# A decoder layer in full fp32 on one core: norm rows by a store and a broadcast load, eleven norms' sums by VectorE, half of the last residual transposed by VectorE, squares placed later

## The chip, the cores and the metric

The kernel runs on one core of a Trainium2 chip. The core has TensorE (PE in the profile, with PEld for its weight loads), VectorE (DVE), ScalarE (ACT), GpSimd (POOL) and SyncE (SP), which here only issues DMAs; POOL and ACT issue some too. Each engine works through its own instructions in order, and semaphores tie the engines together. The metric is the time of one execution in microseconds (us), the median of several.

## The reference, cut to what matters

One layer over 1024 tokens of width 1024: a half feed-forward, a mixer (stick-breaking attention of 16 heads beside a Mamba-2 scan, SSD), cross-attention to 256 memory tokens, and a second half feed-forward. Each part has an RMSNorm ahead of it and one behind it.

```python
def rmsnorm(x, g):
    y = x * lax.rsqrt(jnp.mean(x * x, axis=-1, keepdims=True) + EPS)
    return y * g

f = swiglu(rmsnorm(h, ffn1_pre_g), ffn1_w_gu, ffn1_w_down)
h = h + 0.5 * rmsnorm(f, ffn1_post_g)
m = hybrid_mixer(rmsnorm(h, mix_pre_g), ...)
h = h + rmsnorm(m, mix_post_g)
c = memory_cross_attention(rmsnorm(h, xa_pre_g), rmsnorm(mem, mem_g), ...)
h = h + rmsnorm(c, xa_post_g)
f = swiglu(rmsnorm(h, ffn2_pre_g), ffn2_w_gu, ffn2_w_down)
h = h + 0.5 * rmsnorm(f, ffn2_post_g)
...
# in the mixer: o_att = rmsnorm(o_att, attn_norm_g), and y = rmsnorm(y in 2 groups of 512, ssd_norm_g)
```

## The kernel before, in words

Activations lie transposed: 128 of the 1024 features on the partitions, tokens along the free axis, in two halves of 512 tokens (`hh`), so a half is 8 tiles of 128x512 (`d`). Weights and activations are split into a high and a low part (`split`, L267), and a product is three matmuls (`mm3`, L282: high x high, high x low, low x high). The stages in order, with their rough times: `ffn1` up to 440 us, its down projection to 655 (`down1`, L979, by seven products in place of eight, `down7`, L1019), `ssd` to 1000, `attention` to 1545, `mix_out` to 1672, `xattn` to 1923, `ffn2` up to 2357, its down projection to the end at 2581 (`down_rows`, L1140, again `down7`, with tokens on the partitions).

The norm of one half goes in steps. The squares of its 8 tiles are summed to one 128x512 tile (`sumsq`, L361; the sum is `acc`, `yacc`, `asum` or `bh`), still with features on the partitions. `rms_cols` (L322) sums over partitions with PE: for each block of 128 tokens one matmul with the block as weights and a column of constants (`small`) as the moving side, which gives a 128x4 tile in the PSUM bank `ms`, one column for each block of tokens. ACT takes the root, DVE the reciprocal: the column `c` (`cpost`, `cpre`, `ca`, `cy`, `cmem`). `rms_rows` (L346) turns the column to a row that stands on all 128 partitions: four matmuls with the broadcast column as weights and the identity (`ident`) as the moving side, then a copy by ACT from PSUM (L355) to the row `r` (`rpost`, `rpre`, `rn`, `Ct`, `sq`). Both are matmuls in fp32, which PE makes in several passes.

Who uses which: `post` (L386) closes a stage. It multiplies the result `F` by the row `rpost` and the gain (`apply`, L404, L407), adds the residual `XL` (L411), stores the new residual `h` by POOL (L416), splits it for the next stage (L418, L423), sums the squares of the new residual and makes column and row of the next norm (`cpre`, `rpre`). `pre` (L484) does the latter for the stages that don't spread it. `group_norm` (L1525) makes the columns of the two SSD groups, `keys` (L1548) those of the memory; `mix_row` (L1805), `norm_row` (L2058) and `memory_values` turn these to rows where they are used: in the mixer's output projection, which runs in four passes of 8 tiles (half 0: scan part, attention part; then half 1), each tile's bank is emptied by a product with its row (`mix_sum`, L2003 to L2008).

What sets the order: each engine's instructions are placed by a scheduler in the order of a modelled clock (`self.clock`, which PE's work drives). Work that is put off is listed in `self.later` with a time and runs when the clock has come that far; `pinned` puts a group of matmuls at a given time. DMAs on SP stand in the order in which this places them; an SP transfer that must wait holds all that stand behind it.

In the attention, `vtr` (L1736) turns the values of a pair of heads: DVE transposes 32x32 blocks (`dv`), SP stores to DRAM (`vt<-dv`) and loads back in another order with four DMAs (`dv<-vt`, L1731); `kevac` (L1753) empties the keys and has SP move them by four DMAs (`k<-xl`, L1700).

In the last stage the residual `h`, which lies transposed in DRAM, has to come to tokens on the partitions. POOL loads the 8 tiles of a half (`fetch_h`, L1157), PE transposes 128x128 blocks to two PSUM banks (`shift`, L1160, 8 for each block of 128 tokens), and DVE adds (`end`, L1187, the row at L1190). Half 0 is done while the last products run (`early`, L1201), half 1 behind the last product (`last`, L1241). `ssq` (L1167) takes the squares of a row by ACT, `gain` (L1182) multiplies by the gain on DVE, and the sums of the seven products are gathered at L1080 and L1091.

Of the kernel before, what the change touches and what calls it, by code (L numbers as in the profile page):

```python
# [47 lines left out]
class Kern:  # L48
# [273 lines left out]
    def rms_cols(self, groups, c, ones=None, r2=None):  # L322
# [20 lines left out]
        if r2 is not None:  # L343
            self.kp(nc.vector.tensor_tensor(out=c, in0=c, in1=r2, op=ALU.mult))

# [40 lines left out]
    def post(self, hh, gname, r2, gnext=None, out=None, step=None, spread=True, pins=(23000, 28000), accs=None, at=None, tail=None, hold=False, late=None):  # L386
# [10 lines left out]

        def cols():
            self.rms_cols([accs], c, r2=r2)

        def rows():
            self.rms_rows(c, r)
# [25 lines left out]
        if out is None:  # L428
            self.h[hh] = [self.tc.dram_tile([P, H], F32, name=self.nm(f"h{hh}{d}")) for d in range(KT)]
# [36 lines left out]
        if out is None:  # L466
# [4 lines left out]
            self.held = [lambda: self.rms_cols([accs2], c2)]  # L471
            if not hold:
                q.append((t + t1, self.held.pop()))
            if spread:
                q.append((t + t2, lambda: self.rms_rows(c2[:, :], r2_)))
# [8 lines left out]
    def pre(self, hh, accs, t1, t2):  # L484
        c = self.t(self.rp, [P, 4], F32, f"cpre{hh}", bufs=2)
        r = self.t(self.rp, [P, H], F32, f"rpre{hh}", bufs=1)
        with self.pinned(t1):
            self.rms_cols([accs], c)
        with self.pinned(t2):
            self.rms_rows(c[:, :], r)  # L490
        self.R[hh], self.C[hh] = r, c
# [487 lines left out]
    def down1(self, sp, wdn, act_d, xs_d, gpost, gnext):  # L979
# [15 lines left out]
        def finish(m, i):  # L995
# [5 lines left out]
            elif m == 4:  # L1001
# [4 lines left out]
                self.post(0, gpost, self.C[0], gnext, step=2600, accs=accs[:], tail=(20500, 24000), late=38000)  # L1006
# [10 lines left out]
        self.post(1, gpost, self.C[1], gnext, step=2000, accs=accs[:], at=(6500, 9000, 10000), tail=(7500, 10500))  # L1017
# [122 lines left out]
    def down_rows(self, sp, wdn, act_d, xs_d, out):  # L1140
# [16 lines left out]
        def fetch_h(hh, d):  # L1157
            self.kp(nc.gpsimd.dma_start(out=hs[hh][d], in_=self.h[hh][d]))

        def shift(hh, tb):  # L1160

            xt = [self.t(self.mmp, [P, H], F32, "mm") for _ in range(2)]
            for d in range(KT):
                self.tr(xt[d // 4][:, (d % 4) * P : (d % 4 + 1) * P], hs[hh][d][:, tb * P : (tb + 1) * P])
            return xt

# [34 lines left out]
        def early(tb):  # L1201

            root(0, tb)
            xt = shift(0, tb)
            for dh in range(2):
                end(0, tb, dh, xt)

        def finish(m, tb):
            if m == 2:
# [5 lines left out]
                for d in range(KT):  # L1215
                    at(2500 * d, fetch_h, 0, d)
            elif m == 4:
# [6 lines left out]
                for d in range(KT):  # L1224
                    at(1000 + 2500 * d, fetch_h, 1, d)
            elif m == 5:
                for tb in range(4):
                    at(3000 + 5000 * tb, ssq, 1, tb, 0)
                    at(5000 + 5000 * tb, gain, 1, tb, 0)
# [11 lines left out]
        def last(tb):  # L1241
            xt = shift(1, tb)
# [7 lines left out]
    def ssd(self, close):  # L1250

        nc, ap = self.nc, self.ap
        with self.tc.tile_pool(name=self.nm("ssa"), bufs=1, reuse_waits="tile") as ep, \
# [271 lines left out]
            def group_norm(gr):  # L1525
                c = self.norm_c[gr] = self.t(self.rp, [P, 8], F32, f"cy{gr}")
                self.rms_cols([[y] for y in yacc], c, ones=self.ones512)
# [20 lines left out]
            def keys(n0, n1):  # L1548

                mh, ml, acc, rm = env["mem"]  # L1550
                if n0 == 0:
                    self.mem_c = self.t(self.rp, [P, 2], F32, "cmem")
                    self.rms_cols([[acc]], self.mem_c)
                    yield
                for n in range(n0, n1):
                    ps = yield from self.kvproj(next(W), mh, ml)
                    if n == 0:
                        self.rms_rows(self.mem_c[:, :], rm)
# [88 lines left out]
    def attention(self):  # L1647
        nc, ap = self.nc, self.ap
        with self.pools("at", ["o", "a"], ["w"]) as (op, sp, wsp, pp):
# [52 lines left out]
            def inproj(p):  # L1702
# [12 lines left out]
                def steps(hh, t, before):  # L1715
# [14 lines left out]
                    for q in range(4):  # L1730
                        nc.sync.dma_start(  # L1731
                            out=v[32 * q : 32 * q + 32, :].rearrange("e (j c d) -> e j c d", j=4, c=4), in_=rows[q]
                        )
                    return v
# [49 lines left out]
                vtr(1, tv[1])  # L1784
                kevac(evac((yield from last), 1), h1)

            def before(n):
# [7 lines left out]
                if n == 10:  # L1795
                    late.append(mix_row(0))
                if n == 12:
                    late.pop()()
# [6 lines left out]
            def mix_row(i):  # L1805
                self.mix_r.append(self.t(self.rp, [P, H], F32, f"rpre{i}", bufs=1))
                return self.rms_rows(self.norm_c[i][:, 0:4], self.mix_r[i], tr_tile)
# [109 lines left out]
            def memory_values(mh, ml):  # L1917

                rm = self.t(self.tp, [P, H], F32, "sq1")[:, 0:MEM]
                self.rms_rows(self.mem_c[:, :], rm)  # L1920
# [31 lines left out]
            def beside():  # L1952
                late.append(mix_row(1))
                self.first = self.mix_first(ready.pop())
                for n in range(4 * MIXED):
# [3 lines left out]
                    if n == 2:  # L1959
                        late.pop()()  # L1960
# [10 lines left out]
            self.Wo, self.mix_r, ready, late = self.wstream(wo[0:MIXED]), [], [], []  # L1971
# [38 lines left out]
    def mix_out(self):  # L2010
# [3 lines left out]
        with self.pools("mo", ["r", "a"], ["b"]) as (rp, sp, sp2, dnp):  # L2014
# [43 lines left out]
            def norm_row(i, hh, at):  # L2058
                r = self.t(rp, [P, H], F32, f"rn{i}")
                with self.pinned(self.clock + at):  # L2060
                    self.rms_rows(self.norm_c[i][:, 4 * hh : 4 * hh + 4], r)
# [6 lines left out]
            for n, (hh, part) in enumerate(passes):  # L2068
# [3 lines left out]
                def norms(t):  # L2072
                    c = self.norm_c[2] = self.t(self.rp, [P, 4], F32, "ca", bufs=2)
                    with self.pinned(self.clock + t):
                        self.rms_cols([asum[-1:]], c)
# [33 lines left out]
                if n == 1:  # L2109
                    self.run_later(float("inf"))  # L2110
                    self.post(0, "mix_post_g", None, "xa_pre_g", step=5000, spread=False, accs=ends[0], at=(6000, 11500, 14000), tail=(18000, 0))
                    self.resid(1, 5000, 17000)
                if n == 3:
                    self.flush(0)
                    self.post(1, "mix_post_g", None, "xa_pre_g", step=3000, spread=False, accs=ends[1], at=(6000, 10500, 13000), hold=True)


    def xattn(self):
# [3 lines left out]
        with self.pools("xf", ["a", "b", "w"], []) as (sp, sp2, wsp, pp):  # L2122
# [107 lines left out]
            for s in range(8):  # L2230
# [3 lines left out]
                if s == 4:  # L2234
# [6 lines left out]
                    self.post(0, "xa_post_g", None, "ffn2_pre_g", step=5000, at=(8500, 16000, 19000))  # L2241
# [47 lines left out]
    def run(self):  # L2289
        nc, tc, ap = self.nc, self.tc, self.ap  # L2290
        with tc.tile_pool(name="const", bufs=1) as cp, tc.tile_pool(name="state", bufs=1, reuse_waits="tile") as xp, \
# [6 lines left out]
            self.place(cp, 448)  # L2298
# [17 lines left out]
            def consts():  # L2316
                cst = self.t(self.fp, [P, 2, P], F32, "rpost")
                nc.sync.dma_start(out=cst, in_=ap["consts"])
                nc.scalar.copy(self.ident, cst[:, 0, :])
                nc.scalar.copy(self.tri, cst[:, 1, :])  # L2320
# [41 lines left out]
            self.norm_c = {}  # L2362
# [111 lines left out]
```

## Time and profile before

| | us |
|---|---|
| median of 3 runs | 2585.72 |
| lowest and highest run | 2585.55, 2587.47 |
| the profiled execution's own time | 2583.27 |
| its span, first to last instruction | 2581.5 |
| PE busy | 2564.0 (99%) |
| DVE busy | 2000.7 (78%) |
| ACT busy | 1289.0 (50%) |
| POOL busy | 576.5 (22%) |
| mean granted clock of PE | 0.999 |

A row of a profile's group reads: line, engine, operation, output<-inputs, shapes, how often | busy time in us, mean ns of one | idle time of the engine just ahead, and what ended it. A row of the timeline starts with its start and its duration in us; in brackets stand the idle time ahead of it and what ended that. Records of matmuls overlap, so the price of one is read from starts. A row of windows gives the stretch, its length, the busy time of each engine with its count of instructions, the granted clock (1.00 is full speed), the share of the DMA engines and GB/s.

### The profile page before, as it was taken

Reading aid. Unit: us, or ns where it says so; the run is one execution under the profiler, and the core shown is the slowest. Engines: PE = TensorE matmul, PEld = TensorE weight load, DVE = VectorE, ACT = ScalarE, POOL = GpSimd, SP = SyncE. Lnnn points to the kernel's source line nnn. Section 1 sums busy time; section 2 is a strip of 40 time slices with the busy share of each in tenths; the row PEclk is TensorE's granted clock in tenths of the full one; section 3 lists DMA queues with packets and bytes.
Section 4 is the critical chain, followed back from the end, with each engine's and each line's share of the span. In section 5 each row is a group of like instructions: output and inputs, shape, how many; then the busy total and the mean of one; then the engine's idle time right before and its main releaser. Section 6 shows DMA issues by size and latency. Waiting matters only on the chain. (4 is left out here: it accounts for less than half of the span.)

```text
span 2581.5 us, 36855 instructions
## 1 busy us (share of the span) xinstructions
PE 2564.0 (99%) x12786; PEld 2141.0 (83%) x12786; DVE 2000.7 (78%) x3074; ACT 1289.0 (50%) x2302; POOL 576.5 (22%) x674
## 2 busy tenths in 40 slices
PE   9999999999999999999999999999999999999999
PEld 7888888888787778888888898888888888888887
DVE  7988997779689884787787876876656887777777
ACT  7434444555356663555555654455554433334453
POOL 2555553001000001111111110111012655541000
PEclk9999999999999999999999999999999999999999
DMA  6458988655665516666666655547658443327654
GB/s 240 163 180 293 308 290 305 220 185 166 232 205 197 184 72 212 186 177 160 176 171 152 206 167 202 197 155 260 202 185 304 150 162 111 110 82 237 192 175 147
DMA packets 251628, 498.24 MB, mean 193 GB/s; under 512 B 60592, under 2 KB 69168, under 8 KB 251440
## 3 DMA queue, kind: packets, MB, share of 16 engines
q1 hardware_dynamic: 204176, 387.31, 46.4%
q0 software_dynamic: 23360, 65.03, 8.6%
q10 hardware_dynamic: 23904, 43.53, 4.6%
q8 instruction: 101, 1.65, 0.3%
q14 instruction: 87, 0.71, 0.1%
HBM read 331.65 MB, written 143.13 MB: 184 GB/s over the span
## 5 line engine op out<-in xcount | busy, mean ns | idle before, releaser
L139 PE MATMUL mm<-xh,whi 128*128 128x512 f32 x1312 | 516.7, 403 | 1.1 <-DVE ft L668 0.5
L139 PE MATMUL mm<-xh,wlo 128*128 128x512 f32 x1280 | 491.7, 392 | 0.0
L139 PE MATMUL mm<-xl,whi 128*128 128x512 f32 (+1 forms) x1248 | 485.7, 389 | 0.3 <-DVE xl L277 0.3
L139 PEld LDWEIGHTS mm<-xh,wlo 128*128 128x128 f32 x1280 | 240.6, 188 | 52.4 <-DVE wlo L270 0.5
L139 PEld LDWEIGHTS mm<-xh,whi 128*128 128x128 f32 x1312 | 247.0, 188 | 43.1 <-issue 3.9
L139 PEld LDWEIGHTS mm<-xl,whi 128*128 128x128 f32 x1248 | 235.6, 189 | 33.4 <-DVE xl L277 0.8
L1829 DVE TENSOR_TENSOR_SCAN nb<-nb,begin 128x128 f32<-128x128 f32 (+7 forms) x128 | 172.1, 1347 | 32.3 <-ACT nb L1825 31.9
L1825 ACT ACTIVATE nb<-z,scale 128x128 f32<-128x128 f32 (+2 forms) x192 | 109.5, 580 | 89.5 <-PE z L139 88.6
L270 DVE TENSOR_TENSOR wlo<-wraw,whi 128x1024 fp32r<-128x1024 f32 x61 | 74.6, 1223 | 51.3 <-ACT whi L268 50.9
L268 ACT CAST whi<-wraw 128x1024 fp32r<-128x1024 f32 (+1 forms) x77 | 73.9, 959 | 70.4 <-PE mm L139 43.5
L1846 POOL DMA_DIRECT2D mix<-sq x64 | 53.0, 828 | 248.7 <-DVE sq L1844 181.5
L669 ACT ACTIVATE ft<-ft 128x512 f32<-128x512 f32 x88 | 55.5, 632 | 95.5 <-DVE ft L668 94.9
L139 PE MATMUL dn<-xh,wlo 128*128 128x512 f32 x296 | 101.2, 390 | 0.0
L772 POOL TENSOR_TENSOR wc<-raw,wraw 128x512 f32<-128x512 f32 x55 | 80.7, 1467 | 56.4 <-DVE wlo L270 23.4
L268 ACT CAST ath<-tr 128x512 fp32r<-128x512 f32 (+1 forms) x106 | 57.3, 540 | 66.9 <-PE tr L142 61.9
L772 POOL TENSOR_TENSOR wc<-wraw,raw 128x512 f32<-128x512 f32 x56 | 78.9, 1409 | 52.5 <-DVE whi L270 16.5
L871 POOL TENSOR_TENSOR ft<-ft,e 128x512 f32<-128x512 f32 x37 | 59.7, 1614 | 126.3 <-DVE e L867 51.1
L270 DVE TENSOR_TENSOR atl<-tr,ath 128x512 fp32r<-128x512 f32 (+1 forms) x106 | 66.1, 625 | 28.0 <-ACT ath L268 26.9
L139 PE MATMUL mm<-ath,v 128*128 128x256 f32 x320 | 87.8, 297 | 0.0
L139 PE MATMUL dn<-xh,blk 128*128 128x512 f32 x264 | 85.2, 389 | 0.0
L268 ACT CAST wlo<-wc 128x512 fp32r<-128x512 f32 x79 | 49.1, 621 | 69.2 <-PE dn L139 25.4
L139 PE MATMUL mm<-atl,v 128*128 128x256 f32 x320 | 83.1, 282 | 0.0
(601 smaller groups left out, 6795.2 us busy)
## 6 DMA issues: line engine op xcount, KB each, us to landing
whi<-dwhi SPq DMA_DIRECT2D x82, 512.0 KB, 4.1
wlo<-dwlo SPq DMA_DIRECT2D x82, 512.0 KB, 5.4
wraw<-in_w_gu SPq DMA_DIRECT2D x43, 512.0 KB, 4.0
dwhi<-bh SPq DMA_DIRECT2D x78, 256.0 KB, 4.2
dwlo<-bl SPq DMA_DIRECT2D x78, 256.0 KB, 4.2
raw<-in_w_gu SPq DMA_DIRECT2D x37, 512.0 KB, 4.1
wraw<-xs SPq DMA_DIRECT2D x56, 256.0 KB, 2.9
xs<-ft ACTq DMA_DIRECT2D x54, 256.0 KB, 3.0
```

The lines of the kernel that those rows point to most:

```text
L139: self._pe(self.nc.tensor.matmul(out, lhsT, rhs, start=start, stop=stop, skip_group_check=self.more), cost)
L268: self.kp(self.nc.scalar.copy(hi, src))
L270: self.nc.vector.tensor_tensor(out=lo, in0=src, in1=hi.bitcast(F32), op=ALU.subtract)
L669: nc.scalar.activation(t, t, AF.Silu)
L772: inst = (nc.vector if early else nc.gpsimd).tensor_tensor(out=t, in0=a, in1=b, op=op)
L871: nc.gpsimd.tensor_tensor(out=t1, in0=t1, in1=e, op=ALU.mult)
L1825: nc.scalar.activation(nb[:, s0:s1], z[:, 0:n], AF.Sigmoid, scale=sc[:, i : i + 1])
L1829: nc.vector.tensor_tensor_scan(out=nb[:, 0:Wd][:, ::-1], data0=nb[:, 0:Wd][:, ::-1], data1=begin[:, S - Wd : S][:, ::-1], initial=0.0, op0 ...
L1846: nc.gpsimd.dma_start(out=self.mix_d[p][a * 64 : a * 64 + 64, csl], in_=o, accum_op=ALU.add)
```

## The change

1. Rows. `rms_rows` is replaced in all but a few places: the column is stored to DRAM by SP (`norm<-cpost` and the like, 4-byte pieces), and `row` loads it back with SP as a row that is broadcast to 128 partitions. The load waits until the store has landed. PE still makes the rows of the first norms of the input, of the `post` of half 1 in `ffn1`, and of the norm ahead of `ffn2` of half 1.
2. Sums. For eleven norms (seven tiles of `acc`, four of `yacc`: two groups of the scan in two halves each) `turned` takes the place of `rms_cols`: DVE transposes the sum tile in 32x32 blocks, reduces 32 neighbours to a 128x16 tile, one PE matmul with a constant `quads` (128x32) sums the four quarters of partitions, ACT and DVE take the root and reciprocal, SP stores it, and where the column is needed SP loads it back as 128x4. `quads` is made once by a DVE reduction at the start.
3. Half 0 of the last residual. `fetch_rows` loads it by POOL with four DMAs for each 128x512 tile, in runs of 128 bytes, already so that 32x32 blocks stand where the transposed ones belong; DVE transposes them in place (`turn`). PE's transposes of half 0 and their two banks go. A POOL copy of one column holds each load until a sum tile of the product before is written. The fetches are spread over the first four products.
4. Times. The squares and gains of half 1 in the last stage move from 3000 + 5000 a block to 6500 + 3800; in the attention's first pair of heads the loading back of half 1's values is placed behind `kevac`; one time in `post` of the mixer moves from 13000 to 14000.

The core of the diff:

```diff
     def rms_cols(...):
...
+        if keep:
+            kept = self.tc.dram_tile([nb, P], F32, name=self.nm("norm"))
+            nc.sync.dma_start(out=kept.rearrange("b p -> p b"), in_=c)
+            return kept
+
+    def turned(self, accs, ms, wait=0, c=None):
+        kept = self.tc.dram_tile([4 * len(accs), P], F32, name=self.nm("norm"))
+        ps = self.t(self.msp, [P, H], F32, "ms", bufs=1)
+        for acc in accs:
...
+            self.kp(nc.vector.transpose(acc, acc))
+            self.kp(
+                nc.vector.tensor_reduce(
+                    out=parts[-1][0], in_=acc.rearrange("p (j k) -> p j k", k=32), op=ALU.add, axis=mybir.AxisListType.X
+                )
+            )
+        with self.pinned(self.clock + wait):
+            for n, (part, _) in enumerate(parts):
+                self.mm(ps[0:32, 16 * n : 16 * n + 16], self.quads, part, True, True)
+        for n, (_, x) in enumerate(parts):
+            self.kp(nc.scalar.activation(x, ps[0:32, 16 * n : 16 * n + 16], AF.Sqrt, bias=self.eps[0:32], scale=ms))
+            self.kp(nc.vector.reciprocal(x, x))
+            nc.sync.dma_start(out=kept[4 * n : 4 * n + 4].rearrange("b (q i) -> i (b q)", i=32), in_=x)
+        if c is not None:
+            nc.sync.dma_start(out=c, in_=kept.rearrange("b p -> p b"))
+        return kept
+
+    def row(self, kept, r):
+        self.nc.sync.dma_start(out=r, in_=kept.rearrange("b p -> (b p)").partition_broadcast(P))
...
         def rows():
-            self.rms_rows(c, r)
+            if pe:
+                self.rms_rows(c, r)
+            else:
+                self.row(kept[0], r)
...
+        def fetch_rows(tb, dh, behind):
+            self.kp(nc.gpsimd.tensor_copy(self.scratch, behind[:, 0:1]))
+            rows = self.hall[0].rearrange("(h k) (c e) t -> h e (k c) t", h=2, e=32)[dh]
+            x = hs[0][2 * tb + dh]
+            for q in range(4):
+                t = tb * P + 32 * q
+                out = x[32 * q : 32 * q + 32, :].rearrange("e (c t) -> e c t", t=32)
+                self.kp(nc.gpsimd.dma_start(out=out, in_=rows[:, :, t : t + 32]))
+
+        def turn(tb, dh):
+            x = hs[0][2 * tb + dh]
+            self.kp(nc.vector.transpose(x, x))
...
         def early(tb):
             root(0, tb)
-            xt = shift(0, tb)
             for dh in range(2):
-                end(0, tb, dh, xt)
+                end(0, tb, dh, hs[0][2 * tb : 2 * tb + 2])

         def finish(m, tb):
+            if m < 4:
+                C = (self.F[0][1::2], self.F[1][1::2], self.F[1][0::2], self.F[0][0::2])[m]
+                for dh in range(2):
+                    at(1000 + 6000 * dh, fetch_rows, m, dh, C[2 + dh])
+                    at(16000 + 6000 * dh, turn, m, dh)
...
-                for d in range(KT):
-                    at(2500 * d, fetch_h, 0, d)
...
-                    at(3000 + 5000 * tb, ssq, 1, tb, 0)
-                    at(5000 + 5000 * tb, gain, 1, tb, 0)
+                    at(6500 + 3800 * tb, ssq, 1, tb, 0)
+                    at(8500 + 3800 * tb, gain, 1, tb, 0)
...
-                vtr(1, tv[1])
+                if p:
+                    vtr(1, tv[1])
                 kevac(evac((yield from last), 1), h1)
+                if p == 0:
+                    vtr(1, tv[1]())
...
             def mix_row(i):
                 self.mix_r.append(self.t(self.rp, [P, H], F32, f"rpre{i}", bufs=1))
-                return self.rms_rows(self.norm_c[i][:, 0:4], self.mix_r[i], tr_tile)
+                self.row(self.norm_c[i][0:4], self.mix_r[i])
```

Where the order of instructions moves, three places. On SP in the attention's first pair of heads, before (`k` and `dv` are keys and values of half 1):

```order
L1731 DMA dv_10016<-vt_10014 32x16x32 x4
L1717 DMA mix_130<-ev_10050 128x512
L1727 DMA vt_10057<-dv_10053 128x512
L182 DMA whi_10117<-dwhi_647 128x1024
L1700 DMA k_9855<-xl_2197_9851 64x512
L1731 DMA dv_10059<-vt_10057 32x16x32 x4
L1700 DMA k_9855<-xl_2198_9852 64x512
L1700 DMA k_9856<-xl_2197_9851 64x512
```

and the same place in the changed program:

```order
L1791 DMA vt_10044<-dv_10040 128x512
L182 DMA whi_10104<-dwhi_654 128x1024
L1764 DMA k_9842<-xl_2189_9838 64x512
L1764 DMA k_9842<-xl_2190_9839 64x512
L1764 DMA k_9843<-xl_2189_9838 64x512
L1764 DMA k_9843<-xl_2190_9839 64x512
L1797 DMA dv_10046<-vt_10044 32x16x32 x4
L182 DMA wlo_10105<-dwlo_655 128x1024
```

All four key transfers now stand ahead of the four value loads; before, three stood behind.

On SP in the down projection of `ffn1`, where `post` of half 0 makes its row, before (`raw` and `wraw` are weights and activations of the next steps):

```order
L1044 DMA wraw_6022<-in_w_dn 128x512
L1055 DMA wraw_6022<-xs_1738 128x512
L1044 DMA raw_1327_6033<-in_w_dn 128x512
L1055 DMA raw_1327_6033<-xs_2088 128x512
L1044 DMA wraw_6098<-in_w_dn 128x512
```

and in the changed program:

```order
L1094 DMA wraw_6019<-in_w_dn 128x512
L347 DMA norm_5853<-cpost_5777 128x4x1
L1105 DMA wraw_6019<-xs_1745 128x512
L1094 DMA raw_1326_6030<-in_w_dn 128x512
L1105 DMA raw_1326_6030<-xs_2095 128x512
L378 DMA rpost_5778<-norm_5853 128x512
L1094 DMA wraw_6095<-in_w_dn 128x512
```

The store of the column and the load of the row are new, with three of the stage's loads between them and the rest behind.

On DVE in the last stage, where the sums that PE's banks wait for (`F<-F,dn`) meet the ends of half 0 (`F<-F,st,mm`), before:

```order
L1058 TENSOR_TENSOR wc_25016<-xl_5003_23287,wraw_25013 128x512
L1190 SCALAR_TENSOR_TENSOR F_4956_23240<-F_4956_23240,st_24802,mm_24861 128x512
L1190 SCALAR_TENSOR_TENSOR F_4957_23241<-F_4957_23241,st_24802,mm_24862 128x512
L270 TENSOR_TENSOR whi_24953<-wc_24951,whi_24953 128x512
L270 TENSOR_TENSOR hl_24954<-wraw_24948,hl_24954 128x512
L1080 TENSOR_TENSOR F_4962_23246<-F_4962_23246,dn_24629 128x512
```

and in the changed program:

```order
L1254 SCALAR_TENSOR_TENSOR F_4916_23154<-F_4916_23154,st_24750,xh_4934_23172 128x512
L1254 SCALAR_TENSOR_TENSOR F_4917_23155<-F_4917_23155,st_24750,xh_4935_23173 128x512
L270 TENSOR_TENSOR whi_24817<-wc_24815,whi_24817 128x512
L270 TENSOR_TENSOR hl_24818<-wraw_24812,hl_24818 128x512
L1108 TENSOR_TENSOR wc_24884<-xl_4961_23199,wraw_24881 128x512
L1108 TENSOR_TENSOR wc_24895<-xl_4962_23200,raw_5261_24892 128x512
L270 TENSOR_TENSOR wlo_24828<-wc_24826,wlo_24828 128x512
L270 TENSOR_TENSOR hl_24829<-raw_5245_24823,hl_24829 128x512
L1108 TENSOR_TENSOR wc_24932<-xl_4963_23201,wraw_24929 128x512
L270 TENSOR_TENSOR whi_24886<-wc_24884,whi_24886 128x512
L270 TENSOR_TENSOR hl_24887<-wraw_24881,hl_24887 128x512
L1130 TENSOR_TENSOR F_4922_23160<-F_4922_23160,dn_24583 128x512
```

The two ends of half 0 (they read the transposed residual from SBUF now) stand ten instructions ahead of the first sum instead of three.

111 lines of the change are left out of this document (66 added, 45 removed).

## The prediction

> **What bounds the kernel now.** I read the page first, then the list of waits, then the windows of the stages in which something waits, and at last the timeline around each edit. The page settles the first question:
>
> ```profile
> span 2581.5 us, 36855 instructions
> PE 2564.0 (99%) x12786; PEld 2141.0 (83%) x12786; DVE 2000.7 (78%) x3074; ACT 1289.0 (50%) x2302; POOL 576.5 (22%) x674
> ```
>
> PE (TensorE) is idle for 17.5 us of the span, start and end included, and no other engine is near it. So a microsecond of PE work taken out is a microsecond off the end, unless another engine holds the end of that stage. The waits of PE tell where that is (wait in us, times, longest):
>
> ```profile
> PE z L139 <- DMA k<-xl: 1.9, 1, 1.9
> PE ms L139 <- DVE atl L270: 1.9, 1, 1.9
> PE dn L139 <- ACT dx L268: 0.8, 1, 0.8
> PE dn L139 <- DVE F L1080: 0.8, 1, 0.8
> PE dn L139 <- ACT dn L1091: 0.7, 1, 0.7
> PE dn L139 <- DVE dx L270: 0.5, 1, 0.5
> ```
>
> The two `dx` waits fall together at 646.9 and 648.1 us, at the end of the down projection of the first feed-forward layer (`ffn1`). The windows of that stage (PE, PEld, DVE, ACT, POOL busy) show why:
>
> ```profile
> 608.00:616.00 8.00, 8.00 (x37) 6.61 (x36) 8.00 (x13) 6.18 (x12) 1.62 (x3) 1.00 0.58 196
> 646.00:656.00 10.00, 8.69 (x42) 7.01 (x42) 9.60 (x16) 4.95 (x8) 0.00 (x0) 1.00 0.95 365
> ```
>
> There DVE (VectorE) is as full as PE, all of 8.00 us, and at 646 PE has used up its lead: from 608 to 650 DVE sets the time. Everywhere else PE does. I speak of faster or slower only beyond 0.2% (5.2 us), about what a measurement of this kernel can tell from no change.
>
> **PE work removed.** These are the groups of matmuls that the norms use, and the transposes of the last stage:
>
> ```profile
> L139 PE MATMUL ms<-small,acc 128*128 128x1 f32 x104 | 12.4, 241 | 0.2 <-DVE acc L369 0.2
> L139 PE MATMUL ms<-ident,cpre 128*128 128x128 f32 x48 | 6.4, 277 | 0.0
> L139 PE MATMUL ms<-ident,cpost 128*128 128x128 f32 x48 | 6.3, 274 | 0.0
> L142 PE MATMUL mm<-ident,xh 128*128 128x128 f32 x32 | 4.9, 274 | 0.0
> L142 PE MATMUL mm<-ident,xl 128*128 128x128 f32 x32 | 4.8, 272 | 0.0
> L139 PE MATMUL ms<-small,yacc 128*128 128x1 f32 x32 | 3.8, 248 | 0.0
> L139 PE MATMUL ms<-ident,cy 128*128 128x128 f32 x16 | 2.2, 281 | 0.0
> L139 PE MATMUL ms<-ident,ca 128*128 128x128 f32 x16 | 2.1, 274 | 0.0
> L139 PE MATMUL tr<-ident,cy 128*128 128x128 f32 x16 | 2.1, 274 | 0.0
> L139 PE MATMUL ms<-ident,cmem 128*128 128x128 f32 x8 | 1.3, 287 | 1.9 <-DVE atl L270 1.9
> ```
>
> An L139 matmul in full fp32 leaves two records, so x48 is 24 instructions; the transposes of L142 leave one. The changed program has 4 of the 24 `cpost` left, 12 of the 24 `cpre`, 24 of the 52 `acc`, and none of `yacc` (16), `cy` (8 and 8), `ca` (8), `cmem` (4): 20 + 12 + 28 + 16 + 16 + 8 + 4 = 104 matmuls, 26 groups of four. What one group costs PE is read from starts, since records overlap:
>
> ```profile
> 1559.39 0.95 PE L139 MATMUL ms<-small,asum 128*128 128x1 f32 x8
> ...
> 1560.52 0.40 PE L139 MATMUL dn<-olo,whi 128*128 128x512 f32 x1
> 1560.75 0.40 PE L139 MATMUL dn<-ohi,wlo 128*128 128x512 f32 x1
> ```
>
> One ordinary matmul stands between the first two rows, and ordinary ones follow each other by 0.23: 1560.52 - 1559.39 - 0.23 = 0.90 us for the group. That is 26 x 0.90 = 23.4 us. Of the 64 transposes 32 go. Four of them take 0.44 us:
>
> ```profile
> 2545.82 0.60 PE L142 MATMUL mm<-ident,xh 128*128 128x128 f32 x4
> 2546.26 0.60 PE L142 MATMUL mm<-ident,xl 128*128 128x128 f32 x4
> ```
>
> So 32 x 0.11 = 3.5 us. Added on PE are 11 matmuls with `quads`, 32 rows by 16 columns, of which the trace has none. I bound one between 0.11 (a transpose) and 0.48 (twice what a matmul of such a group costs), and take 0.27, just above the 0.225 of the 128x1 form, whose shape is nearest: 3.0 us, 1.2 to 5.3. PE's net is -23.4 - 3.5 + 3.0 = **-23.9 us**.
>
> **Waits that go.** The longest is at 1037.9: PE waits for the last `k<-xl`. SP issued the first of the four at 1032.02, then this, then the other three:
>
> ```profile
> 1032.62 2.63 SPq L1731 DMA_DIRECT2D dv<-vt  x4
> ```
>
> In the changed order the four `k<-xl` stand ahead of the `dv<-vt`, so the last is issued 2.6 us sooner, more than the wait of 1.9. The wait also cost clock (last columns: granted clock, DMA share, GB/s):
>
> ```profile
> 1038.00:1040.00 2.00, 2.00 (x7) 1.72 (x8) 1.93 (x4) 0.96 (x2) 0.00 (x0) 0.53 0.98 271
> 1040.00:1042.00 2.00, 2.00 (x9) 1.69 (x8) 0.62 (x1) 0.58 (x1) 0.00 (x0) 0.61 0.75 195
> ```
>
> Four microseconds at 0.53 and 0.61 did the work of 2.3, so some 1.7 us go with it, and the term is 1.9 + 1.7 = -3.6 (0 if `k<-xl` is late for another reason than its place). The Trainium skill ("TensorE: Matmul & The Clock Gate", Part 1: The HAM clock gate (the "warmup" mystery)) lets the clock fall only after an idle window of about 3.4 us; here it fell after 1.9. By that rule this term would be 1.9, not 3.6, and the forecast 1.7 us higher; I keep the rows.
>
> The second wait (1.9, `ms` <- DVE `atl`, 1500.18) is the row of the memory's norm waiting for its PSUM bank. The row is loaded by DMA now and needs neither bank nor PE: -1.9. The last stage has 0.75 and 0.66:
>
> ```profile
> 2535.21 1.40 DVE L1190 SCALAR_TENSOR_TENSOR F<-F,st,mm 128x512 f32<-128x512 f32 x2
> 2543.43 0.72 ACT L1171 ACTIVATE sq<-F,cpre 128x512 f32<-128x512 f32 x1
> ```
>
> The two L1190 adds stand ahead of the sums that empty the banks at 2539; in the new order they come seven instructions sooner. The copy that PE waits for at 2544.8 stood behind two squares, and behind one now: -1.4. The `dx` waits stay. Together -3.6 - 1.9 - 1.4 = **-6.9 us**.
>
> **What is added elsewhere.** DVE gets 11 sums by transposing and reducing, and 8 transposes of the residual, at
>
> ```profile
> L1725 DVE STREAM_TRANSPOSE dv<-dv 128x512 f32<-128x512 f32 x16 | 11.2, 700 | 0.3
> L2165 DVE TENSOR_REDUCE st<-dn 128x1 f32<-128x256 f32 x32 | 13.4, 420 | 7.7 <-PE dn L139 7.6
> ```
>
> 0.70 each, and 0.42 for 256 columns, so I estimate 0.70 for 512: 19 x 0.70 + 11 x 0.70 = 21 us. DVE is idle for 580 us of the span, and of the 30 only the sums of `acc` at the end of `ffn1` come where it has no idle time, after the `dx` waits; PE's lead hides nearly all, and for the scan part of `ssd`, where PE's own chain waits on DVE, I allow 0.5 us (0 to 2). Each row now costs a store, its landing and a load that waits for it, both on SP. The nearest rows, small pieces and all, are
>
> ```profile
> dv<-vt SPq DMA_DIRECT2D x64, 64.0 KB, 2.6
> xl<-h POOLq DMA_DIRECT2D x32, 256.0 KB, 5.5
> ```
>
> so 2 x 2.6 = 5.2 us from reciprocal to row at the least, and up to 8 with a wait in the queue; by PE it was under 3 in the first case below. Most rows are asked for well ahead of their use. Two are not. The first is `post` of half 0 in `ffn1`:
>
> ```profile
> 604.67 0.42 SPq L1055 DMA_DIRECT2D wraw<-xs  x1
> 605.63 0.16 DVE L344 TENSOR_TENSOR cpost<-cpost,cpre 128x4 f32<-128x4 f32 x1
> 608.54 1.41 DVE L407 SCALAR_TENSOR_TENSOR F<-F,params,rpost 128x512 f32<-128x512 f32 x2
> ```
>
> The column is ready at 605.8; the store stands on SP ahead of `wraw<-xs`, so this load, issued at 604.67, slips to about 606.2, and the DVE addition that needs it (607.93) to about 609. The row lands at 611 to 612.6, the L407 products move from 608.5 to there, behind four splits. DVE sets the time here, so what it idles comes out at 648, and the 0.9 us of PE taken out at 606 is lost: +1.8 (0 to 3.5). The second is the mixer's output projection, in its second pass and the like one of the fourth:
>
> ```profile
> 1559.66 4.51 SPq L185 DMA_DIRECT2D wraw<-in_w_out  x2
> 1565.73 0.59 ACT L355 COPY rn<-ms 128x512 f32<-128x512 f32 x1 [3.18 <-PE ms L139]
> ```
>
> The row load stands behind the second `wraw`, which is not issued before 1563.8, so the row lands at 1567 to 1570 instead of 1566.3, with the `xl` and `slo` loads behind it. PE fills the three other banks before it needs that one again, which mostly covers it: +1.0 for both (0 to 7). New waits together **+3.3**.
>
> Sum against the profiled execution: 2583.27 - 23.9 - 6.9 + 3.3 = 2555.8 us. That execution lies 2.45 below the median of the runs (2585.72), so I forecast 2558.2, say **2558 us**.
>
> **Rivals.**
>
> *Rows late.* The rows through DRAM miss their dates at the two places, and at the first rows that `ssd` uses, which have the least margin elsewhere. Then the upper ends hold: 3.5 + 7 + 2 = 12.5 instead of 3.3, and some 3 us for `ssd` and for lost clock: 2558 + 12 = 2570. For it speaks the DVE that is full at 608; against it, PE's lead elsewhere.
>
> *POOL's gathers late.* The residual of half 0 now comes in 32 loads of 128-byte runs; each four feed a transpose that stands on DVE 15 us after the first was asked for, and DVE works in order. The price of such an issue is nearest to
>
> ```profile
> L1846 POOL DMA_DIRECT2D mix<-sq x64 | 53.0, 828 | 248.7 <-DVE sq L1844 181.5
> ```
>
> so four issues take 3.3 us and the last lands 5.5 us on, at 9: covered. If a landing took five times 5.5, 27 us, DVE would wait 3 + 27 - 15 = 15 us at each of 8 transposes. Its lead on PE is five steps of twelve matmuls, 5 x 12 x 0.23 = 13.8 us, so some 2 to 3 us would show at each, and the clock falls with it: some 24 us, 2582. `xl<-h` ran through POOL beside a busy DVE and landed at 5.5, so the trace speaks against it. The Trainium skill ("SBUF — State Buffer", SBUF: two separate sides) speaks for it: while DVE runs its two-port modes GpSimd cannot write descriptors, and a load of about 620 ns takes about 3100.
>
> *Slower: SP stops.* SP works in order, and 36 new transfers stand on it: 16 stores that wait for a reciprocal, 20 loads that wait for a store to land. If the weight loads behind each of the 16 pairs came late by as much as the wait at 1037.9, 16 x 3.6 = 58 us would be added: 2616. From 27.5 / 16 = 1.7 us a pair on nothing is left of the gain. Against it: weights are loaded at least one tile ahead, and SP waited often before, with PE idle for only 17.5 us in all.
>
> **How the numbers follow.** Forecast 0.74; rows late 0.17; gathers late 0.05 (half of it within 0.2%, half still faster); SP stops 0.04 (0.03 of it slower, 0.01 within). The low end is the sum with no new wait and `quads` at 1.2 us, 2558.2 - 3.3 - 1.8 = 2553.1, and 1 us for the price of a group, which I read at one place: 2552. The high end is the late rows with `quads` at 5.3: 2572; what is beyond it is less than 2 in 10. Faster by over 0.2%: 0.74 + 0.17 + 0.025, 0.93; within it 0.025 + 0.01, 0.04; slower 0.03.
>
> **What would show it.** Right: PE's busy time near 2540, a span near 2554; no wait at `k<-xl` and no clock under 0.9 after it; `ms` <- `atl` gone; the `dx` waits near 648 longer than 1.3 us together. Wrong: PE idle over 25 us, with `rpost`, `rn` or `F` at L449 or L2074 behind its waits (rows late), with `xh`/`xl` transposes in the last stage (gathers), or with weight tiles (SP).

## The result, and the profile after

The change made the kernel slower: 2657.18 us (5 runs, 2652.13 to 2658.61) against 2585.55, a ratio of 1.0273 with an interval of 1.0258 to 1.0289. The forecast was 2558, faster. The page of the changed kernel, first its span and busy times:

```profile
span 2650.3 us, 36531 instructions
PE 2572.3 (97%) x12568; PEld 2132.0 (80%) x12568; DVE 2020.7 (76%) x3107; ACT 1283.6 (48%) x2289; POOL 596.3 (22%) x706
```

PE is idle for 2650.3 - 2572.3 = 78.0 us, where it was 17.5. And it is busy for longer although 104 matmuls and 32 transposes are gone, so part of the busy time must be slow. Summed over windows of 2 us (busy time of PE x (1 - granted clock), wherever the clock is under 0.98), the clock took this:

| profiled execution | span | PE idle | lost to a slow clock | PE's work at full clock |
|---|---|---|---|---|
| before | 2581.5 | 17.5 | 1.7 | 2562.3 |
| after | 2650.3 | 78.0 | 28.1 | 2544.2 |
| difference | +68.8 | +60.5 | +26.4 | -18.1 |

So PE's work went down as the change meant, and idle time and slow clock took nearly five times as much back (86.9 us). PE's list of waits, in which no row was above 1.9 us, now begins

```profile
PE dn L139 <- DVE sq L2074: 9.7, 2, 5.5
PE ms L139 <- DVE cpost L344: 7.7, 1, 7.7
PE mm L139 <- DMA wlo<-dwlo: 7.7, 3, 5.1
PE dn L139 <- ACT pt L268: 6.6, 1, 6.6
PE dn L139 <- DVE ft L1130: 5.7, 1, 5.7
PE mm L139 <- DVE dg L1625: 5.3, 1, 5.3
PE dn L139 <- DVE wlo L270: 4.5, 3, 4.0
```

Neither the wait at `k<-xl` nor that of `ms` on `atl` is there any more. What the new ones have in common shows in the list of DMAs (queue, how many, KB each, median us from issue to landing):

```profile
rpost<-norm SPq DMA_DIRECT2D x5, 256.0 KB, 5.2
norm<-root SPq DMA_DIRECT2D x11, 2.0 KB, 7.3
cpre<-norm SPq DMA_DIRECT2D x4, 2.0 KB, 3.7
norm<-cpost SPq DMA_DIRECT2D x2, 2.0 KB, 10.3
```

A store of 2 KB takes 7.3 to 10.3 us to land, longer than the weight loads of 512 KB (medians of 3.7 to 5.6). I had taken 2.6. DVE waits 77 us in all for rows and columns from DRAM (none came that way before); the two longest rows of its list are

```profile
DVE F L449 <- DMA rpost<-norm: 28.6, 4, 14.5
DVE scale L1732 <- DMA cpre<-norm: 22.3, 2, 11.2
```

How that reaches PE is read at the end of `ffn1`'s down projection. On SP the store (L371), two weight loads, and the two loads of the column and the row, which wait for the store:

```profile
669.65 0.33 SPq L371 DMA_DIRECT2D norm<-root  x1
670.44 0.55 SPq L182 DMA_DIRECT2D whi<-dwhi  x1
671.08 0.38 SPq L182 DMA_DIRECT2D wlo<-dwlo  x1
676.34 0.37 SPq L373 DMA_DIRECT2D cpre<-norm  x1
676.76 0.50 SPq L378 DMA_DIRECT2D rpre<-norm  x1
```

on DVE the first instruction that needs the column, and on PE a row that has nothing to do with that norm, but whose column stands behind it on DVE:

```profile
680.87 0.17 DVE L1732 TENSOR_SCALAR scale<-cpre 128x4 f32<-128x4 f32 x1 [11.25 <-DMA cpre<-norm]
```

```profile
683.34 2.05 PE L139 MATMUL ms<-ident,cpost 128*128 128x128 f32 x8 [7.70 <-DVE cpost L344]
...
685.61 0.63 PE L139 MATMUL mm<-xl,whi 128*128 128x512 f32 x1
686.04 0.63 PE L139 MATMUL mm<-xh,wlo 128*128 128x512 f32 x1
```

From the store to its use it is 680.87 - 669.65 = 11.2 us; DVE works in order and stands still for all of it; PE uses up its lead and waits 7.7 us; and then its matmuls follow each other by 0.43 us instead of 0.23. The windows give the clock for that (the last three columns are granted clock, DMA share and GB/s):

```profile
680.00:684.00 4.00, 0.66 (x3) 0.69 (x4) 1.44 (x6) 0.30 (x1) 0.00 (x0) 0.50 0.14 47
684.00:688.00 4.00, 4.00 (x14) 3.42 (x14) 1.46 (x3) 1.03 (x2) 0.18 (x1) 0.50 0.00 0
```

Not every delay is a row that is late. At the place in `ffn1` that the prediction worked out, these are SP's transfers and DVE's instructions:

```profile
605.68 0.38 SPq L347 DMA_DIRECT2D norm<-cpost  x1
...
606.91 0.33 SPq L1094 DMA_DIRECT2D raw<-in_w_dn  x1
607.29 0.43 SPq L1105 DMA_DIRECT2D raw<-xs  x1
614.64 0.32 SPq L378 DMA_DIRECT2D rpost<-norm  x1
```

```profile
609.21 0.69 DVE L270 TENSOR_TENSOR hl<-wraw,hl 128x512 fp32r<-128x512 f32 x1
618.41 0.69 DVE L1108 TENSOR_TENSOR cb<-xl,raw 128x512 f32<-128x512 f32 x1 [8.52 <-DMA raw<-in_w_dn]
...
619.91 1.41 DVE L449 SCALAR_TENSOR_TENSOR F<-F,params,rpost 128x512 f32<-128x512 f32 x2 [0.21 <-DMA rpost<-norm]
```

DVE's 8.5 us here end with `raw`, an ordinary load that was issued at 606.9, 1.2 us behind the store, and the row comes in that load's shadow. This one load (first line) took 11.4 us to land; the same load in the kernel before (second line, issued at 607.03) took 3.0:

```profile
raw<-in_w_dn SPq DMA_DIRECT2D x1, 256.0 KB, 11.4
raw<-in_w_dn SPq DMA_DIRECT2D x1, 256.0 KB, 3.0
```

So there were two suspects, a row that is late and a store that holds up what is behind it, and a third: SP, which issues nothing from 607.7 to 614.6.

### The profile page after: what moved, and what is told of

It is laid out like the page before. It is cut to its first block, busy times and chain, and to the rows that moved or that the text cites. A ratio compares the mean times of both kernels' runs of the same rounds, so it can differ in the third digit from the quotient of the medians.

```text
span 2650.3 us, 36531 instructions
## 1 busy us (share of the span) xinstructions
PE 2572.3 (97%) x12568; PEld 2132.0 (80%) x12568; DVE 2020.7 (76%) x3107; ACT 1283.6 (48%) x2289; POOL 596.3 (22%) x706
## 5 line engine op out<-in xcount | busy, mean ns | idle before, releaser
L270 DVE TENSOR_TENSOR atl<-tr,ath 128x512 fp32r<-128x512 f32 (+1 forms) x107 | 67.2, 629 | 29.0 <-ACT ath L268 28.1
L139 PE MATMUL dn<-xh,whi 128*128 128x512 f32 x240 | 82.7, 389 | 0.0
```

The lines of the kernel that those rows point to most:

```text
L139: self._pe(self.nc.tensor.matmul(out, lhsT, rhs, start=start, stop=stop, skip_group_check=self.more), cost)
L270: self.nc.vector.tensor_tensor(out=lo, in0=src, in1=hi.bitcast(F32), op=ALU.subtract)
```

## The experiments

All are compared with runs of the kernel before on the same chip; the chips differ between experiments (the kernel before had medians of 2582.7 to 2585.2 on them), so differences between two experiments are good to 2 or 3 us. The kernels made from the changed one keep its last stage. Where an edit changes a DMA, the builder can also place other instructions in another order, and where that bears on a reading it is said.

**compact: the same change, stores in runs of 128 bytes.** DVE transposes the small tile of reciprocals before it is stored, so the store is 16 runs of 128 bytes (the plain columns likewise, in four DMAs):

```diff
-            self.kp(nc.vector.reciprocal(x, x))
-            nc.sync.dma_start(out=kept[4 * n : 4 * n + 4].rearrange("b (q i) -> i (b q)", i=32), in_=x)
+            self.kp(nc.vector.reciprocal(x[:, 0:16], x[:, 0:16]))
+            self.kp(nc.vector.transpose(x, x))
+            nc.sync.dma_start(out=kept[4 * n : 4 * n + 4].rearrange("b (q i) -> (b q) i", i=32), in_=x[0:16])
```

> The changed kernel, with one edit: DVE transposes each norm's column tile in 32x32 blocks before SP stores it, so the store goes in runs of 128 bytes (16 of them) instead of 512 pieces of 4 bytes. Theory A (the store of 4-byte pieces lands after 7 to 10 us, so each row is ready some 13 us after its reciprocal, DVE stands in order, PE waits 4 to 8 us and the clock halves behind it): the store lands in about 2.6 us, PE's long waits fall from 57 us to about 15 and the loss by clock from 28 to about 7, time 2657 - 42 - 21 = about 2594. Theory B (the landing is long because the transfers queue behind the weight loads, whatever the pieces): the store still takes 7 us or more, time about 2655. Theory C (DVE's added transposes and reductions are what PE waits for): a few small DVE instructions more, 2657 or slower.

Measured: 2581.31 us, ratio 0.9979 (0.9969 to 0.9989), which is 76 us under the changed kernel. Its span, its longest waits, and the place above:

```profile
span 2576.1 us, 36573 instructions
PE 2547.5 (99%) x12568; PEld 2114.9 (82%) x12568; DVE 2025.6 (79%) x3128; ACT 1283.0 (50%) x2289; POOL 596.1 (23%) x708
```

```profile
PE ms L139 <- DVE cpost L344: 3.9, 1, 3.9
PE dn L139 <- DVE F L1136: 3.1, 1, 3.1
```

```profile
665.43 0.32 SPq L377 DMA_DIRECT2D norm<-part  x1
...
667.76 0.37 SPq L379 DMA_DIRECT2D cpre<-norm  x1
```

The load that waits for the store is issued 2.3 us behind it, where it was 6.7 (over the twelve places where a load follows its own store: 2.8 us in the mean, where it was 8.7). PE is idle for 28.6 us and loses 4.5 to the clock. So storing in larger pieces takes away the whole loss against the kernel before, though not yet to the forecast; theories B and C fall. A part of it can be order: ahead of `ffn2`, SP issues a weight load (`wlo<-dwlo`) ahead of the row's load here and behind it in the changed kernel, where PE then waits 5.1 us for that weight.

**poolq: stores and loads of the norms issued by POOL, still in 4-byte pieces.**

```diff
-            nc.sync.dma_start(out=kept.rearrange("b p -> p b"), in_=c)
+            nc.gpsimd.dma_start(out=kept.rearrange("b p -> p b"), in_=c)
...
-        self.nc.sync.dma_start(out=r, in_=kept.rearrange("b p -> (b p)").partition_broadcast(P))
+        self.nc.gpsimd.dma_start(out=r, in_=kept.rearrange("b p -> (b p)").partition_broadcast(P))
```

> The changed kernel, with the stores and loads of the norms issued by POOL instead of SP; the stores stay in 4-byte pieces. Theory A with the rows as the cause: the rows are as late as before, PE's waits behind DVE products with rows stay, only the three waits on weights (wlo, and the raw tiles in the first down projection, 18 us) go with their clock: about 2630. Theory D (the harm is SP standing still: weights behind it come late): nearly all waits go, below 2580.

Measured: 2671.1 us, ratio 1.033 (1.031 to 1.0349). SP is free, and nothing is gained, not even what I expected of the weights:

```profile
PE dn L139 <- DVE sq L2074: 17.4, 3, 9.2
PE ms L139 <- DVE cpost L344: 9.7, 1, 9.7
...
PE mm L139 <- DMA wlo<-dwlo: 6.1, 3, 4.8
```

The loss does not need SP to stand still (D falls); here POOL stands in its place until a store has landed.

**rows_only: rows through DRAM, all sums and columns by PE.** `turned` is replaced by `rms_cols`.

> The changed kernel without the sums by DVE: all columns are made by PE as in the kernel before, only the rows go through DRAM (and the last stage as changed). Theory A: rows as late as in the changed kernel, but the columns no longer come through DRAM, so the waits at 683 us and 1758 us (cpre) go: about 2657 - 12 - 8 + 7 of PE work = 2644. Theory C (DVE's added sums): most of the loss goes, near 2575.

Measured: 2663.8 us, ratio 1.0315 (1.0282 to 1.0348). The sums by DVE are not the harm. The wait at `cpost`, which I expected to go with the column's load, is 8.5 us here: DVE's product with the row `rpre` stands ahead of it just the same, and that step of the expectation was wrong.

**last_stage: the kernel before, with only the last stage's part and the order of keys and values.**

> The kernel before, with only the last stage's part of the change (half 0 of the residual gathered by POOL and transposed by DVE, squares and gains later) and the four key transfers ahead of the value loads in the attention. All theories: PE's 32 transposes go (3.5 us), the waits at 1037.9 with its slow clock (3.6) and at 2539.8 and 2544.8 (1.4): 2585.6 - 8.5 = about 2577. If POOL's gathers are late, PE waits show in the last 220 us and the time is 2580 or more.

Measured: 2582.01 us, ratio 0.9986 (0.9977 to 0.9996), a gain of 3 us where 8.5 were expected. The longest of PE's waits:

```profile
PE mm L139 <- DMA wlo<-dwlo: 2.1, 1, 2.1
```

The wait for `k<-xl` is gone, and at 1064.8 PE waits 2.1 us for a weight that SP issued at 1058.2: more than half of that term was given back. That the moved transfers made this weight late is not shown. The gathers on POOL are on time; nothing on PE waits for them.

**late_rows: compact, with two more copies from DRAM to DRAM between store and load.**

```diff
+        for _ in range(2):
+            again = self.tc.dram_tile([nb, P], F32, name=self.nm("norm"))
+            self.nc.sync.dma_start(out=again, in_=kept)
+            kept = again
```

> The compact kernel (stores in 128-byte runs) with two more copies from DRAM to DRAM, 2 KB each in long runs, between each norm's store and its loads, so that a row is as late as in the changed kernel, without any store of 4-byte pieces. Theory A (lateness of the row is what costs): the extra copies land after about 2.3 us each and what the queue adds, 5 to 6 us more, so PE's long waits and the slow clock come back: 2640, between 2620 and 2660. Theory E (512 pieces of 4 bytes clog the DMA engines for other transfers): about 2582, as the compact kernel.

Measured: 2619.43 us, ratio 1.0138 (1.0121 to 1.0154): 38 us over compact, with no 4-byte store in it. The same places wait:

```profile
PE ms L139 <- DVE cpost L344: 7.6, 1, 7.6
PE dn L139 <- DVE sq L2089: 7.4, 2, 4.3
```

Late rows cost without any small store, 38 us where A expected 58, just outside its range. A load follows its store by 8.9 us in the mean, so the rows are as late as in the changed kernel (8.7). But this is not the changed kernel with late rows alone: its order moved too. Ahead of `ffn2` DVE's first product with `rpost` stands two products later and waits 2.3 us for its row, where it waits 14.5 in the changed kernel; in all DVE waits 39 us for rows and columns here and 77 there. So 38 us is not the price of lateness in the changed kernel's own order.

**store_only: last_stage, with 17 stores of columns in 4-byte pieces that nobody reads.** All rows and columns are PE's.

```diff
+        if self.h[0][0] is not self.x0:
+            kept = self.tc.dram_tile([nb, P], F32, name=self.nm("norm"))
+            nc.sync.dma_start(out=kept.rearrange("b p -> p b"), in_=c)
```

> The kernel last_stage (rows and columns all by PE as in the kernel before) with a store of each norm's column to DRAM by SP in 4-byte pieces added, 17 of them, which nobody reads. Theory A: nothing waits for them: 2582 to 2588. Theory E (traffic of 4-byte pieces): most of the loss stays, 2610 or more.

Measured: 2614.85 us, ratio 1.0118 (1.0098 to 1.0137): 33 us over last_stage, for 37 KB that nobody waits for. Theory A is not the whole, and E holds here. 38 + 33 = 71 of the 76 us between the changed kernel and compact (41 + 34 = 75 by the ratios), but that the loss is made of these two halves is inferred from the sum: each was measured in another kernel. The landing of transfers on both queues tells how (last_stage, then store_only):

```profile
whi<-dwhi SPq DMA_DIRECT2D x82, 512.0 KB, 4.2
h<-F POOLq DMA_DIRECT2D x36, 256.0 KB, 2.9
```

```profile
whi<-dwhi SPq DMA_DIRECT2D x82, 512.0 KB, 5.4
h<-F POOLq DMA_DIRECT2D x36, 256.0 KB, 4.6
norm<-cpre SPq DMA_DIRECT2D x6, 2.0 KB, 10.5
```

`h<-F` isn't on SP, and it is slowed by 1.7 us in the median. In the changed kernel the same two medians are 4.6 and 2.6, so `h<-F` isn't slowed there; but the three loads behind its store at 605.7 (`wraw<-xs`, `raw`, `raw<-xs`) land after 11.4 to 11.7 us, as they do here (10.9 to 11.2). So this harm is in the changed kernel too; how much of the 76 us it makes there is not measured.

**store_16: the same stores in 128 pieces of 16 bytes** (`out=kept` with `kept` of shape [P, nb]).

> As store_only (the rows and columns by PE, a store of each column to DRAM by SP that nobody reads), but each store goes in 128 pieces of 16 bytes instead of 512 of 4; the bytes are the same. Theory F (each piece takes the DMA engines a fixed time, and all transfers behind it wait): a quarter of the pieces, so a quarter of the 33 us that store_only lost to last_stage: about 2590. Theory G (SP stands still for its stores, whatever their pieces): 2610 or more.

Measured: 2580.91 us, ratio 0.9994 (0.9984 to 1.0004). Nothing of the 33 us is left, where F expected a quarter:

```profile
h<-F POOLq DMA_DIRECT2D x36, 256.0 KB, 2.8
norm<-cpre SPq DMA_DIRECT2D x6, 2.0 KB, 2.4
```

This is the cleanest pair: store_only and store_16 have the same instructions in the same order on every engine, and the three loads behind the store at `ffn1` land after 4.2 to 4.5 us here.

**store_pool: the 512-piece stores of store_only, issued by POOL.**

> As store_only, with the 512-piece stores issued by POOL instead of SP. Theory F: the pieces go through the same DMA engines, so weights behind them come late all the same: 2605 to 2615. Theory G (SP stands still): SP has none of these stores, so the loss is gone: 2582 to 2588.

Measured: 2615.27 us, ratio 1.0131 (1.0113 to 1.0149). The whole 33 us stay with SP free of them: what is held up is not held up by SP's standing (G falls).

**store_16_apart: 128 pieces of 16 bytes, 512 bytes apart in DRAM** (`out=kept[:, 0:nb]` with `kept` of shape [P, P]).

> As store_16 (128 pieces of 16 bytes, nobody reads them), but the pieces go to places 512 bytes apart in DRAM, as the 4-byte pieces of the changed kernel do, instead of side by side. Theory F (a price for each piece, some 10 us / 512 = 0.02 us): as store_16, the store lands in 2.4 to 3.1 us and the time is about 2581. Theory H (it is the scattered writing to DRAM): landing of 5 us or more, 2590 or more.

Measured: 2580.42 us, ratio 0.998 (0.9971 to 0.999), `norm<-cpre` lands in 2.3 us.

**store_4_close: 512 pieces of 4 bytes, side by side in DRAM** (stored from a tile with a gap behind each column).

> As store_only (512 pieces of 4 bytes, nobody reads them), but the pieces go side by side in DRAM; the source is a tile in which each column has a gap behind it, which takes one small DVE copy more a norm. Theory F: 512 pieces all the same, landing of about 10 us, 2610 to 2620. Theory H (scattered writing): landing of about 2.5 us, about 2583.

Measured: 2611.27 us, ratio 1.0099 (1.0084 to 1.0115):

```profile
norm<-twice SPq DMA_DIRECT2D x14, 2.0 KB, 9.6
```

So it is not where the pieces go (H falls): the same 2 KB land in 9.6 us in 512 pieces of 4 bytes and in 2.3 in 128 of 16.

**compact_pe_sums: compact, with all sums by PE again.**

> The compact kernel with all sums over partitions by PE again (rows still through DRAM in 128-byte runs): it prices the part of the change that moves eleven sums to DVE, once rows are early. PE gets 11 groups of 0.90 back for 11 quads matmuls of 0.2 each: +7.7 us; the columns no longer come through DRAM, so the wait of 3.9 at 675 us with its slow clock (2) goes: 2581.3 + 7.7 - 5.9 = 2583. If DVE's added work cost more than that, below 2580.

Measured: 2581.17 us, ratio 0.9991 (0.9981 to 1.0001), the same as compact within the runs (2581.31). The eleven sums on DVE bring nothing that these runs can tell. By the two profiles PE's work at full clock is 3.9 us less with them (2543.1 against 2547.0), where I had taken 7.7, and its idle time is the same (28.6 and 28.7); the wait at `cpost` fell by 2.1 us, not by 3.9. These two profiled executions lie 3.4 us below and 4.2 above the medians of their runs, so where the 3.9 went is not shown.

**mended: compact, with `ffn1`'s own rows and its two sums by PE.** The calls of `post` in `ffn1` get `pe=True, pe2=True`, and `pe2` keeps `cpre` and `rpre` on PE:

```diff
-                q.append((t + t2, lambda: self.row(kept[1], r2_)))
+                q.append((t + t2, lambda: self.rms_rows(c2[:, :], r2_) if pe2 else self.row(kept[1], r2_)))
```

> The compact kernel, with the four rows and two columns that the first feed-forward layer makes given back to PE (its DVE has no idle time, and the first scan product waits for the column): PE gets 3 rows of 0.90 and 2 sums of 0.90 back for two quads matmuls of 0.2, +4.1; the waits at 645 and 675 us (0.9 and 3.9) and their slow clock (4.5) go: 2581.3 + 4.1 - 9.3 = 2576. If it is 2580 or more, what is left of the compact kernel's loss lies elsewhere.

Measured: 2573.99 us, ratio 0.9967 (0.9954 to 0.998), faster than both kernels, with the clock full throughout:

```profile
span 2570.4 us, 36625 instructions
PE 2546.5 (99%) x12604; PEld 2118.0 (82%) x12604; DVE 2019.4 (79%) x3120; ACT 1283.3 (50%) x2291; POOL 596.5 (23%) x708
```

## Why the prediction was wrong, point by point

**The step that failed** is the price of a row's way through DRAM: "The nearest rows, small pieces and all, are" `dv<-vt`, 2.6 us, "so 2 x 2.6 = 5.2 us from reciprocal to row at the least, and up to 8". `dv<-vt` is a load in 128-byte runs; the column's store goes in 4-byte pieces and landed in 7.3 to 10.3. SP issued the load 6.2 to 11.6 us behind the store, and with the load's own 4 to 5 us a row came some 10 to 17 us behind its store. That PE's lead would hide a row "asked for well ahead of its use" fell with it, in the scan, the mixer, the cross-attention and before `ffn2` alike. The upper end of my range for the price was no bound: no row of the trace showed a store in such pieces, and I bounded it by loads.

The Trainium skill ("DMA: Bandwidth & Descriptors", Rules for kernel authors) says that a last dimension that isn't contiguous becomes one descriptor for each element and should be rearranged to be contiguous. The traces agree for SP: store_only has 9744 DMA packets more than last_stage, 573 a store, and store_16 has 2448, 144 a store (both from the pages' counts, 252011, 261755 and 254459); issued by POOL the same stores show only 32 packets each (252555 in store_pool), so there the count can't tell. That rule spoke against this change, and I had weighed two others.

**A cost that the prediction did not have**: a store in 512 pieces of 4 bytes slows the transfers around it, whoever issues them (33 us, store_only and store_pool, against store_16). I priced a transfer only by what waits for it.

**The clock.** I priced it at the wait that goes and not at those that come. It took 26.4 us more than before, beside 60.5 of idle time.

**The rivals.** "Rows late" named the mechanism and two of its places, the mixer's output projection and the scan, and its signs came (PE idle far over 25 us, with L2074 behind its waits); but it had 0.17, and put the time 12 us over the forecast, where the kernel came out 99 over it. "SP stops" came out on the right side for the wrong reason: in poolq and store_pool SP does not stand for the stores, and the loss stays. "POOL's gathers late" did not happen (the 32 loads landed in medians of 3.5 and 4.4 us); there the trace had been read rightly against the rule of the Trainium skill that the prediction cites.

**What held.** PE's work fell by 18.1 us at full clock, where 23.9 was forecast; a `quads` matmul was cheaper than 0.27 (x22 records, 2.2 us), so the 0.90 for a group, read at one place, must have been too much as a mean. DVE's prices were right, 0.70 and 0.68 against 0.70 and 0.70:

```profile
L359 DVE STREAM_TRANSPOSE acc<-acc 128x512 f32<-128x512 f32 x7 | 4.9, 705 | 0.1
L361 DVE TENSOR_REDUCE part<-acc 128x16 f32<-128x512 f32 x7 | 4.8, 679 | 0.1
```

The waits at `k<-xl` and `atl` went, though last_stage shows that the first came back at a weight load as 2.1 of its 3.6 us. In `ffn1` I expected the loss at 648 us; it came at 629.6, as a wait of 5.7, and the `dx` waits were as before (0.8 and 0.5).

**What the idea is worth** shows in mended: 2574.0 us against 2583.6 for the kernel before on the same chip, 10 us, where I had put 27 for the change. By the profiles it is 2581.5 - 2570.4 = 11.1 of the 27.5. Of the 16.4 between, 4.1 is PE's work given back, 4.0 the PE term that was too large (15.8 saved for 19.8), and the other 8.3 idle time: 23.9 us against 17.5 before, where I had put 1.9 less (5.2 of waits gone without their clock, 3.3 new).

**What stays open.** How the loss of 76 us divides between late rows and slowed transfers, as said at store_only. Whether the count of the pieces or their size sets the price of a store: no run stored 512 pieces of 16 bytes. The other stores of the same runs speak for the size: in store_only 256 pieces of 4 bytes (`norm<-cmem`) landed in 10.1 us and 1024 (`norm<-cy`) in 10.3, no sooner and no later than 512, while in store_16 128 pieces of 8 bytes (`cmem`) took 4.8 and of 32 bytes (`cy`) 3.1. So theory F's fixed time for each piece does not hold at 4 bytes. Why other transfers wait is open too: in the changed kernel from 608 to 616 the DMA engines were busy for 16 to 25% and moved 25 to 43 GB/s, with three loads under way, so they were not full. Loads are not like stores: 512 pieces of 128 bytes landed in 2.6 (`dv<-vt`) and 512 of 4 bytes in 3.7 (`cpre<-norm`).

## What to carry to other kernels

Price a new transfer by a row of the same direction and the same size of pieces, not of the same bytes; where the trace has none, that is an unknown to be bounded upward, and it is worth a look at how many pieces the access pattern makes. A small store whose result isn't needed can still cost, by what it delays on every queue, and a late operand costs on an engine that works in order all that stands behind it, and then the clock. Here the mending was one small DVE transpose ahead of the store, and leaving the rows on PE where the consumer has no slack.

## What the runs showed of the hardware that I had not expected

- A store of 2 KB from SBUF to DRAM lands in 7.3 to 11 us in 512 pieces of 4 bytes and in 2.3 to 3.0 in 128 of 16 bytes (medians), each side by side or apart in DRAM, the 4-byte ones from SP and POOL alike.
- With 17 such stores of 4-byte pieces in the kernel, 256 KB stores on another queue land in a median of 4.6 us instead of 2.9 (store_only), and at the one place read, in `ffn1`, loads of 256 KB issued right behind one in 10.9 to 11.7 instead of 4.2 to 4.5 (store_only and the changed kernel, against store_16).
- The clock does not follow the length of one wait: behind a wait at the same matmul, for its weight, it fell to 0.50 in store_16 (2.08 us, at 1061.5) and stayed at 1.00 in last_stage (2.06 us, at 1064.8). In compact it stayed full behind the 3.1 us at 2536 and stood at 0.50 from 648 on, behind waits of 0.9, 0.2 and 0.5 within 5 us. The Trainium skill ("TensorE: Matmul & The Clock Gate", Part 1: The HAM clock gate (the "warmup" mystery)) has a window that runs free of the program, which fits that the same wait can fall either way; its 3.4 us of idle time before the clock falls does not fit these rows.
